# One core, matmul with RMS norm: four warming matmuls, and two products, two transposes, two block loads and two closing steps moved

## The chip, the cores and the metric

The kernel runs on one core of one Trainium2 chip. The metric is the device time of one execution in microseconds (us); the time before is the median of three runs. TensorE (PE) multiplies into eight PSUM banks, VectorE (DVE) and ScalarE (ACT) work on tiles in SBUF and read PSUM, GpSimd (POOL) issues the loads that change type, SyncE (SP) issues the stores and the DMA transposes.

## What is computed

```python
def reference(a, b, gamma, eps):          # a: 2048 x 2048, b: 2048 x 2048, fp32
    x = np.matmul(a, b)
    rms = np.sqrt(np.mean(x ** 2, axis=-1, keepdims=True) + eps)
    return (gamma * x / rms).astype(np.float32)
```

## The kernel before

Rows of A are cut into 16 blocks of 128, columns of B into four chunks of 512 (a left half and a right half, `j` = 0 and 1), the inner dimension into 16 tiles of 128, taken in 8 pairs (`kp`). The order of every engine's instructions is the order in which they are written, by hand: nothing is rescheduled. Each engine works through its own list and waits by semaphore for what another has to finish.

**Seven products for eight.** Two row blocks times one half of B make a 2 x 2 problem, which is done by a Strassen scheme of seven products, each 8 matmuls of 128x128 by 128x512 (`product`, L362; `product_matmul`, L350). Products 1, 2 use A's upper quarters, 4 its lower right one, 5, 6, 7, 3 use sums of quarters, numbered 1, 2, 3, 4 in `a_sums` (L328); B's sums are made by `b_diff` and `b_rest` (L340, L343). A product either starts a PSUM bank (1 and 7) or adds on top of what the bank holds. Between products that share a bank, ScalarE copies the bank to where the sum so far is wanted. Later groups do the same once more over two groups (`step`, L389).

**Stages.**
- Head: rows 0 to 3, left half, while B's left half streams in; plain matmuls (L406), A transposed on TensorE by `transpose_first` (L167) and `transpose_head` (L178). Ahead of it eight warming matmuls on zeros (L163).
- Right half of the head (`stream_right`, L472): rows 0 and 1 plain in acc[0] to acc[3] (`plain`), rows 2 and 3 (`PAIR`) by products: 1 and 6 and later 4 in `u2` = acc[4], 2 and 5 in `u4` = acc[5], 7 in `p7` = acc[6], 3 in acc[0]. B's last tile is used in the last step, `kp` = 7.
- Between (L515 to L561): the four banks of rows 0, 1 are evicted (L445); blocks 4 and 5 are normed on ScalarE (`row_norm`, L220), scaled to fp16 on VectorE (`row_factor`, `row_apply`, L230 to L243), turned on TensorE in two halves each (`transpose_half`, L191, into tbank and another bank) and copied out (`take_transposed`, L201). `pair_ends` (L556) then joins the banks of rows 2, 3: two ScalarE copies and three VectorE adds, the last of which reads acc[0].
- Groups of two blocks, 4 and 5 first: each half of each group is one segment, numbered `n`. `do(n, m)` (L572) issues product m and its copy, in the banks

```python
B1, B2, B3, B7 = (acc[1], acc[0]), acc[3:5], (acc[6], acc[5]), acc[2]
```

where the first index is `n % 2`: product 1 goes to B1, 4 and 6 to B2, 3 and 5 to B3, 7 to B7. `first_segment` (L607) is n = 0, `segment` (L638) and `block_segment` (L712) the next, `last_group` (L752) the blocks 14 and 15 together. `finish(r)` (L306) multiplies a row block by its inverse and gamma on VectorE and issues the store on SP. `square_half`, `square_right` (L275, L296) take the sums of squares on ScalarE.
- Blocks from 6 on are loaded by POOL (`load_block`, L132; two buffers), after a wait in POOL's own list (`wait_for`, L145), and `prepare` (L245) scales them on VectorE and turns them by DMA transposes on SP's queue.

Of the kernel before, what the change touches and what calls it, by code (L numbers as in the profile page):

```python
# [17 lines left out]
def kernel(  # L18
# [13 lines left out]
    nc = tc.nc  # L32
    P = 128
# [63 lines left out]
    def copy_on(engine):  # L97
        return nc.scalar.copy if engine == "A" else nc.vector.tensor_copy
# [60 lines left out]
    identity_h = consts.tile([P, P], FP16, name="identity_h")  # L159
    nc.vector.tensor_copy(out=identity_h, in_=identity_f)  # L160

    for _ in range(8):
        nc.tensor.matmul(acc[0], warm[:, 0:P], warm[:, 0:CH], start=True, stop=True)  # L163

    def transpose_first():  # L167
        bank = [tbank, acc[6]]
        view = [b.rearrange("p (r m) -> p r m", r=HB) for b in bank]
        for t in range(2):  # L170
            for r in range(HB):
                nc.tensor.matmul(view[t][:, r, :], a0f[:, r, t * P:(t + 1) * P], identity_f,
                                 is_transpose=True, start=(r == 0), stop=(r == HB - 1))
        for t, copy in enumerate((nc.vector.tensor_copy, nc.scalar.copy)):
            for h in range(2):
                copy(out=head_at[:, t, 2 * h:2 * h + 2, :], in_=view[t][:, 2 * h:2 * h + 2, :])
# [88 lines left out]
    def x_chunk(mb, c):  # L265
        return x_tile(mb, c // 2)[:, (c % 2) * CH:(c % 2 + 1) * CH]
# [94 lines left out]
    def product(g, j, m, bank, start=True):  # L361
        for kp in range(KP):  # L362
            product_matmul(g, j, m, bank, kp, start)
# [81 lines left out]
            copy_on(engine)(out=x_chunk(*g), in_=banks[g])  # L445

    transpose_first()
    for kp in range(KP):
        if kp + 4 < KP:
            load_head(kp + 4)  # L450
        else:
            load_later(1)
        before = [lambda: transpose_head(kp + 1)] if kp + 1 < KP else []
        if kp == KP - 2:
            before.append(lambda: a_sums(PAIR, (3,), False))
        stream(kp, before, len(groups1) + {0: 5, 1: 3}.get(kp, 2))
        if kp == KP - 1:
            evict(groups1, "ADADADA")
        stream_in_parts(last1, kp)
        if kp > 0:  # L460
            b_diff(0, kp - 1)
        if 0 < kp < KP - 2:
            b_rest(0, kp - 1)
# [8 lines left out]
    def stream_right(kp):  # L472
        first, second = ([(g, 2 * kp + t) for g in plain] for t in range(2))
        if kp == 0:
            for both in zip(first, second):
                for g, kt in both:
                    head_matmul(banks[g], *g, kt)
            product_matmul(PAIR, 1, 1, u2, kp, True)
            product_matmul(PAIR, 1, 2, u4, kp, True)
            return  # L480
        product_matmul(PAIR, 1, 1, u2, kp, True)
        for g, kt in first:
            head_matmul(banks[g], *g, kt)
        if kp == KP - 1:
            product_matmul(PAIR, 1, 7, p7, kp - 1, True)
        product_matmul(PAIR, 1, 2, u4, kp, True)
        if kp < KP - 1:
            product_matmul(PAIR, 1, 7, p7, kp - 1, True)
        for g, kt in second:
            head_matmul(banks[g], *g, kt)  # L490

    for kp in range(KP):
        load_later(1)
        b_diff(1, kp)
        stream_right(kp)
        if kp % 2 == 0:
            square_half(kp // 2, 0)
        if kp > 0:
            b_rest(1, kp - 1)
        if kp == 0:  # L500
            b_diff(0, KP - 1)
            b_rest(0, KP - 3)
        if kp == 1:
            b_rest(0, KP - 2)
            b_rest(0, KP - 1)
        if kp in (2, 3, 4):
            a_sums(PAIR, ((1,), (2,), (4,))[kp - 2])
# [4 lines left out]

    r2, r3 = HB - 2, HB - 1  # L515
    x11, x12, x21, x22 = (x_chunk(r, c) for r in (r2, r3) for c in (2, 3))
    copy_on("A")(out=x11, in_=u2)
    product_matmul(PAIR, 1, 7, p7, KP - 1, True)
    b_rest(1, KP - 1)
    add(x11, u4, x11)  # L520
    evict(plain[:1], "A")
    row_norm(HB)
    row_norm(HB + 1)
    product(PAIR, 1, 6, u2, start=False)
    nc.vector.tensor_copy(out=u4, in_=u2)
    row_factor(HB)
    row_apply(HB)
    evict(plain[1:2], "D")
    row_factor(HB + 1)
    row_apply(HB + 1)  # L530
    evict(plain[2:3], "A")
    product(PAIR, 1, 3, acc[0])
    product(PAIR, 1, 5, u4, start=False)
    turned = [transpose_half(HB, h, (tbank, acc[1])[h]) for h in range(2)]
    take_transposed(HB, 0, turned[0], nc.scalar.copy)
    take_transposed(HB, 1, turned[1], nc.vector.tensor_copy)
    load_block(HB + 3)
    for r in range(HB):
        take_pre(r)
    square_right(0)  # L540
    evict(plain[3:], "A")
    square_right(1)

    def turn(h):
        view = transpose_half(HB + 1, h, (tbank, acc[2])[h])
        take_transposed(HB + 1, h, view, nc.vector.tensor_copy)

    for kp in range(KP):
        if kp == 6:
            turn(0)  # L550
        product_matmul(PAIR, 1, 4, u2, kp, False)
    turn(1)
    load_block(HB + 4)
    a_sums(G0, (3, 1, 2), False)

    def pair_ends():  # L556
        nc.scalar.copy(out=x22, in_=p7)
# [49 lines left out]
    def first_segment():  # L607
        n, g, j = 0, G0, 0
        nxt = 2 * g + 2
        do(n, 1)  # L610
        do(n, 7, False)
        finish(0, (1,))
        pair_ends()
        do(n, 2)
        row_norm(nxt)
        a_sums(g, (4,))
        finish(0, (0,))
        do(n, 6)
        do(n + 1, 1)
        prepare(nxt)  # L620
        do(n, 5)
        nc.scalar.copy(out=chunks(n)[2], in_=B7)
        take(n, 22)
        row_norm(nxt + 1)
        take(n, 11)
        finish(1)
        do(n, 4)
        take(n, 21)
        prepare(nxt + 1)
        square_half(2 * g + 1, j)  # L630
# [7 lines left out]
    def segment(n):  # L638
        g, j = halves[n]
        ra, rb, nxt = 2 * g, 2 * g + 1, 2 * g + 2  # L640
        more = g + 1 < NG
        if g >= G2 and (g - G2) % 2 == 1 and j == 0:
            block_segment(n)
            return
        first = g >= G2 and (g - G2) % 2 == 0
        do(n, 6)
        if j == 0:
            finish(ra - 1)
            row_norm(nxt)
        elif g == G0:  # L650
            square_right(r2)
        do(n - 1, 3)
        take(n - 1, 12)
        if j == 0:
            square_right(ra - 2)
            prepare(nxt)
            a_sums(g, (4,))
            finish(ra - 2)
        else:
            if not first:  # L660
                square_half(ra, 0)
            if g == G0:
                square_right(r3)
                finish(r2, (1, 0))
            elif g == G0 + 1:
                finish(r3, (1,))
            elif g == G2:
                b_two(4)
            elif not first and g > G2:
                finish(ra - 2)  # L670
        if g < G2:
            do(n, 2)
            take(n, 11)
        if g == G2 - 1 and j == 1:
            b_two(3)
            b_two(1)
        do(n + 1, 1)
        if j == 1 and g + 2 < NG:
            wait_for(at(nxt + 1)[:, KT - 1, 0:1])
            if g > G0:  # L680
                load_block(nxt + 2)
                wait_for(a32[nxt + 2][:, 0:1])
            load_block(nxt + 3)
        if j == 1:
            if first:
                a_two_sums(g)
            a_sums(g + 1, (1, 2))
        do(n, 7)
        if j == 0:
            row_norm(nxt + 1)  # L690
        if j == 1:
            a_sums(g + 1, (3,))
        do(n, 5)
        take(n, 22)
        if j == 1:
            take_pre(rb)
            if not first:
                take_pre(ra)
        do(n, 4)
        take(n, 21)  # L700
        if j == 0:
            square_half(rb, 0)
            prepare(nxt + 1)
            if g == G2:
                b_two(2)
        else:
            if not first:
                square_right(rb)
            if g == G0:
                finish(r3, (0,))  # L710

    def block_segment(n):  # L712
# [11 lines left out]
        square_right(ra - 1)  # L724
        add(x00, W2, x00)
        prepare(nxt)
        do(n + 1, 1)
        take(n - 1, 12)
        square_half(ra - 2, 0)
# [22 lines left out]
    def last_group():  # L752
# [51 lines left out]
        do(n, 7)  # L804
        add(x22[0], x21[0], x22[0])
        add(b2[0], b2[0], x21[0])
        square_of(rb, x22[0])
        add(x11[1], x11[1], gam[2], ALU.mult)
        do(n + 1, 5)
        nc.scalar.copy(out=x22[1], in_=b3[1])  # L810
        wide = a_pool.tile([P, K], FP32, name="a32")
        chunk = [wide[:, c * CH:(c + 1) * CH] for c in range(NCH)]
        add(chunk[1], x22[0], gam[1], ALU.mult)
# [40 lines left out]
        r_b = inverse(root(last_sq, part))  # L854
        nc.vector.tensor_scalar_mul(out=xb[:, 0:CH], in0=xb[:, 0:CH], scalar1=r_b)
        nc.sync.dma_start(out=rows(rb, 0, CH), in_=xb[:, 0:CH])
        for c in (1, 3):
            by_r(chunk[c], r_b)
        scaled_gamma(chunk[2], b2[1], r_b, gam[2])
        nc.sync.dma_start(out=rows(rb, CH, N), in_=wide[:, CH:])  # L860

# [38 lines left out]
```

## Time and profile before

| what | value |
|---|---|
| median of three runs | 219.25 us (218.78 to 219.85) |
| the profiled execution | 219.36 us |
| its span, first to last instruction | 217.6 us |
| around the span | 1.76 us |
| mean granted TensorE clock | 0.990 |
| instructions | 2966 |
| first, last start of a TensorE matmul | 1.46, 210.18 us |
| HBM read, written | 34.60 MB, 16.78 MB |

A row of the timeline is: start, duration, engine, line and operation, output<-inputs, shapes, count, and in brackets how long the engine had been idle and what ended that. Rows of one kind that follow one another are merged (x8). PE is a matmul, PEld the load of its weights. A matmul of 512 columns is shown with 0.38 us, since its end is modelled; what it costs in a stream is the distance to the next start. "Who waited for whom" gives the engine and line, what it waited for, the sum, the count and the longest. In the row of slices, each digit is the busy share of a fortieth of the span in tenths.

### The profile page before, as it was taken

Reading aid. Unit: us, or ns where it says so; the run is one execution under the profiler, and the core shown is the slowest. Engines: PE = TensorE matmul, PEld = TensorE weight load, DVE = VectorE, ACT = ScalarE, POOL = GpSimd, SP = SyncE. Lnnn points to the kernel's source line nnn. Section 1 sums busy time; section 2 is a strip of 40 time slices with the busy share of each in tenths; the row PEclk is TensorE's granted clock in tenths of the full one; section 3 lists DMA queues with packets and bytes.
Section 4 is the critical chain, followed back from the end, with each engine's and each line's share of the span. In section 5 each row is a group of like instructions: output and inputs, shape, how many; then the busy total and the mean of one; then the engine's idle time right before and its main releaser. Section 6 shows DMA issues by size and latency. Waiting matters only on the chain.

```text
span 217.6 us, 2966 instructions
## 1 busy us (share of the span) xinstructions
PE 207.6 (95%) x1016; PEld 95.9 (44%) x1016; DVE 161.6 (74%) x323; ACT 113.3 (52%) x223; POOL 35.3 (16%) x74
## 2 busy tenths in 40 slices
PE   7899999999999999999999999999999999999970
PEld 3344544444455444444444444444444444444420
DVE  1227769999899997788975899399856985475771
ACT  2110001910599579498626962594728951555772
POOL 7644434434001000100021001100101000000020
PEclk9999999999999999999999999999999999999996
DMA  7999999999969798978674975497596992040454
GB/s 151 167 200 204 203 205 209 209 211 211 399 220 358 295 264 230 334 294 240 163 234 167 350 246 99 184 245 240 118 268 237 326 261 50 0 193 3 193 191 195
DMA packets 37039, 46.60 MB, mean 214 GB/s; under 512 B 22560, under 2 KB 26656, under 8 KB 35744
## 3 DMA queue, kind: packets, MB, share of 16 engines
q0 software_dynamic: 10608, 23.86, 45.5%
q1 hardware_dynamic: 26144, 22.29, 33.7%
q10 hardware_dynamic: 272, 0.26, 0.3%
q8 instruction: 8, 0.13, 0.2%
q14 instruction: 7, 0.06, 0.1%
HBM read 34.60 MB, written 16.78 MB: 236 GB/s over the span
## 4 chain that ended last, share of the span: by engine, by line
PE 85%; DMA 9%; POOL 2%; issue 1%; ACT 1%; ACTq 0%; DVE 0%; POOLq 0%
PE acc L358 65%; PE acc L406 11%; DMA early<-in_a_dram 5%; DMA b<-in_b_dram 4%; PE acc L397 3%; PE tbank L397 2%; POOL b L115 1%; PE tbank L358 1%; PE tbank L435 1%; PE tbank L182 1%; POOL early L119 1%; PE tbank L195 0%; PE acc L195 0%; ACT a L766 0%; ACTq L895 0%
## 5 line engine op out<-in xcount | busy, mean ns | idle before, releaser
L358 PEld LDWEIGHTS <-s 128*128 128x128 f16 (+1 forms) x312 | 30.5, 98 | 37.0 <-DVE s L335 0.3
L272 ACT ACTIVATE sq<-x 128x1024 bf16<-128x1024 f32 (+1 forms) x33 | 33.2, 1005 | 24.8 <-DVE x L101 20.9
L406 PE MATMUL acc<-b,head_at 128*128 128x512 bf16 x176 | 43.0, 379 | 0.9 <-DMA b<-in_b_dram 0.7
L311 DVE SCALAR_TENSOR_TENSOR x<-x,r,gamma_sb 128x1024 f32<-128x1024 f32 x28 | 34.9, 1282 | 0.5
L358 PE MATMUL acc<-b,head_at 128*128 128x512 bf16 x136 | 33.9, 379 | 0.0
L101 DVE TENSOR_TENSOR x<-acc,x 128x512 f32<-128x512 f32 x33 | 22.3, 687 | 11.4 <-PE acc L358 5.4
L358 PEld LDWEIGHTS <-head_at 128*128 128x128 f16 (+1 forms) x192 | 18.7, 98 | 22.2
L358 PE MATMUL acc<-b,at_even 128*128 128x512 bf16 x112 | 26.3, 379 | 0.0
L406 PEld LDWEIGHTS <-head_at 128*128 128x128 bf16 x176 | 16.9, 98 | 20.1 <-issue 1.0
L358 PE MATMUL acc<-early,s 128*128 128x512 bf16 x104 | 25.5, 379 | 0.0
L358 PE MATMUL acc<-b,s 128*128 128x512 bf16 x104 | 24.6, 379 | 0.0
L358 PEld LDWEIGHTS <-at_even 128*128 128x128 f16 x160 | 15.6, 98 | 18.6
L224 ACT ACTIVATE sq<-a 128x1024 bf16<-128x1024 f32 x22 | 23.3, 1058 | 0.6 <-DMA a<-in_a_dram 0.2
L358 PE MATMUL acc<-t_left,s 128*128 128x512 bf16 x96 | 22.7, 379 | 0.0
L115 POOL DMA_DIRECT2D b<-in_b_dram x32 | 17.2, 541 | 20.4 <-DMA b<-in_b_dram 14.3
L445 ACT COPY x<-acc 128x512 f32<-128x512 f32 x7 | 4.0, 581 | 25.8 <-PE acc L406 25.8
L587 ACT COPY acc<-acc 128x512 f32<-128x512 f32 x12 | 6.9, 576 | 10.4 <-PE acc L358 10.4
L187 DVE COPY head_at<-tbank 128x1024 bf16<-128x1024 bf16 x7 | 4.8, 691 | 8.1 <-PE tbank L182 8.1
L293 DVE RECIPROCAL r<-rms 128x1 f32<-128x1 f32 x16 | 2.6, 160 | 10.6 <-ACT rms L288 10.6
L101 DVE TENSOR_TENSOR x<-tbank,x 128x512 f32<-128x512 f32 x9 | 6.2, 690 | 4.2 <-PE tbank L435 4.1
L589 ACT COPY x<-acc 128x512 f32<-128x512 f32 x10 | 5.9, 585 | 5.3 <-PE acc L358 5.3
L769 POOL TENSOR_SCALAR x<-x,r 128x512 f32<-128x512 f32 x2 | 1.4, 691 | 41.9 <-DVE r L293 41.9
(129 smaller groups left out, 240.5 us busy)
## 6 DMA issues: line engine op xcount, KB each, us to landing
out_dram<-x SPq DMA_DIRECT2D x29, 512.0 KB, 3.0
a<-in_a_dram POOLq DMA_DIRECT2D x9, 1024.0 KB, 5.5
b<-in_b_dram POOLq DMA_DIRECT2D x32, 256.0 KB, 9.9
a<-in_a_dram POOLq DMA_DIRECT2D x4, 512.0 KB, 10.0
early<-in_a_dram POOLq DMA_DIRECT2D x7, 256.0 KB, 10.2
gamma_sb<-in_gamma_dram POOLq DMA_DIRECT2D x2, 512.0 KB, 10.1
head_at<-in_a_dram POOLq DMA_DIRECT2D x1, 1024.0 KB, 8.2
out_dram<-x SPq DMA_DIRECT2D x3, 256.0 KB, 2.6
```

What stands on the lines that cost most here:

```text
L101: nc.vector.tensor_tensor(out=out, in0=in0, in1=in1, op=op)
L115: nc.gpsimd.dma_start(out=raw[j][kp][:, t, :], in_=b[lo:lo + P, j * HALF:(j + 1) * HALF])
L187: nc.vector.tensor_copy(out=head_at[:, 2 * kp:2 * kp + 2, :, :], in_=view)
L224: nc.scalar.activation(out=junk, in_=a32[mb][:, h * HALF:(h + 1) * HALF], func=ACTF.Square, scale=2.0 ** -8, accum_out=n2[:, h:h + 1])
L272: nc.scalar.activation(out=sq[:, 0:src.shape[-1]], in_=src, func=ACTF.Square, scale=inv_sqrt_n, accum_out=msq[mb][:, c:c + 1])
L311: nc.vector.scalar_tensor_tensor(out=x, in0=x, scalar=inverse_of[mb], in1=gamma_sb[:, h * HALF:(h + 1) * HALF], op0=ALU.mult, op1=ALU.mult)
L358: nc.tensor.matmul(bank, lhsT[:, kp, :], rhs, start=(start and kp == 0), stop=(kp == KP - 1), skip_group_check=not start)
L397: nc.tensor.matmul(bank, lhsT[:, k, :], rhs, start=(m in (1, 7) and k == 0), stop=(k == KQ - 1), skip_group_check=m not in (1, 7))
L406: nc.tensor.matmul(bank, head_at[:, kt, r, :], head_rhs(c, kt), start=(kt == 0), stop=(kt == KT - 1))
L445: copy_on(engine)(out=x_chunk(*g), in_=banks[g])
L587: nc.scalar.copy(out=b3, in_=b2)
L589: nc.scalar.copy(out=chunks(n)[2], in_=B7)
```

## The change

1. Four more warming matmuls follow `transpose_first`.
2. In the last step of `stream_right`, product 6's first four matmuls, and the copy out of `u2` that they need, come ahead of product 2's last matmul, which uses B's last tile. The other four stay behind.
3. Product 4 of rows 2, 3 is issued in three parts: two matmuls ahead of block 4's transposes, four behind them, two behind block 5's transposes. VectorE scales block 5 behind its copy of block 4's second half; ScalarE evicts the last plain bank ahead of row 0's square.
4. Block 5's transposes, product 4's last part, block 8's load and the three sums of A go behind the first group's product 1; row 1's square goes there too. Product 2 of that group is issued ahead of product 7.
5. Block 14 is loaded as soon as block 12 is transposed, and normed and prepared one segment earlier, at the end of (g = 5, j = 1); block 15 takes block 14's old place in (g = 6, j = 0).
6. In `last_group` a square on ScalarE goes behind the copy that followed it, and two scalings of 512 columns become one instruction over both.

The counts of all other instructions are the same. The diff, without its context:

```diff
+    def busy(times):
+        for _ in range(times):
+            nc.tensor.matmul(acc[0], warm[:, 0:P], warm[:, 0:CH], start=True, stop=True)
+    busy(8)
...
     transpose_first()
+    busy(4)
...
         if kp == KP - 1:
+            copy_on("A")(out=x11, in_=u2)
             product_matmul(PAIR, 1, 7, p7, kp - 1, True)
+            for k in range(4):
+                product_matmul(PAIR, 1, 6, u2, k, False)
         product_matmul(PAIR, 1, 2, u4, kp, True)
...
-    copy_on("A")(out=x11, in_=u2)
...
-    product(PAIR, 1, 6, u2, start=False)
+    for kp in range(4, KP):
+        product_matmul(PAIR, 1, 6, u2, kp, False)
...
     row_factor(HB + 1)
-    row_apply(HB + 1)
     evict(plain[2:3], "A")
     product(PAIR, 1, 3, acc[0])
     product(PAIR, 1, 5, u4, start=False)
+    def product_4(lo, hi):
+        for kp in range(lo, hi):
+            product_matmul(PAIR, 1, 4, u2, kp, False)
+    product_4(0, 2)
     turned = [transpose_half(HB, h, (tbank, acc[1])[h]) for h in range(2)]
     take_transposed(HB, 0, turned[0], nc.scalar.copy)
     take_transposed(HB, 1, turned[1], nc.vector.tensor_copy)
+    row_apply(HB + 1)
     load_block(HB + 3)
     for r in range(HB):
         take_pre(r)
+    evict(plain[3:], "A")
     square_right(0)
-    evict(plain[3:], "A")
-    square_right(1)
-    def turn(h):
-        view = transpose_half(HB + 1, h, (tbank, acc[2])[h])
-        take_transposed(HB + 1, h, view, nc.vector.tensor_copy)
-    for kp in range(KP):
-        if kp == 6:
-            turn(0)
-        product_matmul(PAIR, 1, 4, u2, kp, False)
-    turn(1)
-    load_block(HB + 4)
-    a_sums(G0, (3, 1, 2), False)
+    product_4(2, 6)
+    def turn_next():
+        for h in range(2):
+            view = transpose_half(HB + 1, h, (tbank, acc[2])[h])
+            take_transposed(HB + 1, h, view, nc.vector.tensor_copy)
...
         do(n, 1)
+        square_right(1)
+        turn_next()
+        product_4(6, KP)
+        load_block(HB + 4)
+        a_sums(g, (3, 1, 2), False)
+        do(n, 2)
         do(n, 7, False)
         finish(0, (1,))
         pair_ends()
-        do(n, 2)
...
+        own = nxt + (g == NG - 2)
         if j == 0:
             finish(ra - 1)
-            row_norm(nxt)
+            row_norm(own)
...
-            prepare(nxt)
+            prepare(own)
...
-            if g > G0:
+            if G0 < g < NG - 3:
                 load_block(nxt + 2)
                 wait_for(a32[nxt + 2][:, 0:1])
             load_block(nxt + 3)
...
-        if j == 0:
+        if j == 0 and g < NG - 2:
             row_norm(nxt + 1)
         if j == 1:
             a_sums(g + 1, (3,))
+            if g == NG - 3:
+                row_norm(nxt + 2)
...
-            prepare(nxt + 1)
+            if g < NG - 2:
+                prepare(nxt + 1)
...
+            if g == NG - 3:
+                prepare(nxt + 2)
...
         prepare(nxt)
+        load_after(at(nxt)[:, KT - 1, 0:1], nxt + 2)
         do(n + 1, 1)
...
-        square_of(rb, x22[0])
         add(x11[1], x11[1], gam[2], ALU.mult)
         do(n + 1, 5)
         nc.scalar.copy(out=x22[1], in_=b3[1])
+        square_of(rb, x22[0])
...
-        for c in (1, 3):
-            by_r(chunk[c], r_b)
+        by_r(wide.rearrange("p (c n) -> p c n", n=CH)[:, 1::2, :], r_b)
```

## The prediction

> **What bounds the kernel now.** I read the page's shares first, then who waited on TensorE, the chain that ended last, and the timeline where the edits fall. Shares, and three of the slices:
>
> ```profile
> PE 207.6 (95%) x1016; PEld 95.9 (44%) x1016; DVE 161.6 (74%) x323; ACT 113.3 (52%) x223; POOL 35.3 (16%) x74
> PE   7899999999999999999999999999999999999970
> DVE  1227769999899997788975899399856985475771
> PEclk9999999999999999999999999999999999999996
> ```
>
> TensorE is full from the second slice to the last but one, at full clock; VectorE has long full stretches too. All that TensorE waited for:
>
> ```profile
> PE acc L163 <- DVE pace L155: 1.5, 1, 1.5
> PE acc L406 <- DMA b<-in_b_dram: 0.7, 1, 0.7
> PE tbank L435 <- DVE head_at L187: 0.4, 1, 0.4
> PE tbank L182 <- DMA early<-in_a_dram: 0.2, 1, 0.2
> ```
>
> The last of these is at 26.02 us. In the chain:
>
> ```profile
> 15.19 10.79 DMA early<-in_a_dram
> ...
> 67.09 70.79 PE acc L358 x328
> ```
>
> So the kernel is input DMA up to 26.02, then matmuls one behind the other (216 ns a step, 1.726 for a product of eight) up to 210.6, with one hole that the list is too coarse for (203.49, below), then 7 us of ending. An edit between 26 and 210 can gain almost nothing; it can only open a hole. The question at each is what still covers it.
>
> **Part 1, four more warming matmuls.** The first head matmuls run 6.11 to 7.78 and the next waits until 8.51 for B (the 0.7 above). Four at 216 ns are 0.86: they start near 5.85, so the seven head matmuls run 6.72 to 8.23 and still meet the wait. Cost 0, cover left 0.28. At half clock (427 ns, as the warming ones at 1.46 to 4.85) they are 1.71, less the hole of 1.1 between 7.41 and 8.51: at most 0.6. Below nothing: a hole of 1.1 left the clock at full, so nothing is saved here.
>
> The Trainium skill's page "TensorE: Matmul & The Clock Gate", Part 1, speaks against this edit: the gate opens after about 3.4 us of sustained work, in a window that runs free, so more matmuls behind an open gate buy nothing. The trace agrees: granted clock 1.00 in every stretch from 10 us on. By the row the four cost 0, by the rule with the gate a window later the 0.6 above. The same section closes the gate after an idle window of about 3.4 us; the stall of part 4 is shorter, so by the rule it costs no clock either.
>
> **Part 2, half of product 6 ahead.** It needs its bank copied first: ScalarE's copy (L517) runs 56.06 to 56.65 and the moved matmuls start at 56.94. Cover 0.29, cost 0. B's last tile is then needed 4 x 216 ns = 0.86 later. VectorE starts on that tile at 56.64 and TensorE at 56.94: no wait to remove here. But the head matmuls end 0.86 later, so ScalarE's eviction and both row norms do: norm 4 ends at 61.58 (60.71), norm 5 at 64.13 (63.27). VectorE's block 4 scaling then ends at 63.60 (62.87), after block 4's transposes began (63.42); two matmuls of product 4 put ahead move those to 63.85. Cost 0; without that cover 0.2.
>
> **Part 3, block 4.** The first group's product 1 writes the bank of the second turned half. That half's transposes start at 64.30 and end at 64.91; VectorE's copy runs 64.95 to 65.64, now ahead of block 5's scaling. TensorE arrives, after four more matmuls of product 4, at 64.74 + 0.86 = 65.61 and goes on 0.05 after the copy (as at L435: copy to 11.21, matmul at 11.26), at 65.69. Cost **0.08**. Queued behind the copy is block 5's scaling, to 66.85; its transposes are now wanted at 67.42, so it is covered.
>
> **Part 4, block 5 behind product 1, 2 ahead of 7.** This is where I see a new wait. Product 1 of the next half (n = 1) starts in acc[0], where product 3 of rows 2, 3 lies until `pair_ends`' last add (72.83 below):
>
> ```profile
> 66.48 0.61 PE L195 MATMUL acc<-identity_h,a_first 128*128 128x128 f16 x8
> ...
> 67.13 0.69 DVE L202 COPY at_even<-acc 128x1024 f16<-128x1024 f16 x1
> 67.86 0.69 DVE L335 TENSOR_TENSOR s<-at_even 128x1024 f16<-128x1024 f16 x1
> ...
> 68.59 0.69 DVE L335 TENSOR_TENSOR at_even<-at_even 128x1024 f16<-128x1024 f16 x1
> ...
> 69.31 0.69 DVE L335 TENSOR_TENSOR s<-at_even 128x1024 f16<-128x1024 f16 x1
> ...
> 70.11 1.28 DVE L311 SCALAR_TENSOR_TENSOR x<-x,r,gamma_sb 128x1024 f32<-128x1024 f32 x1
> ...
> 72.83 0.69 DVE L101 TENSOR_TENSOR x<-acc,x 128x512 f32<-128x512 f32 x1
> ...
> 73.84 1.46 PE L358 MATMUL acc<-b,at_even 128*128 128x512 bf16 x6
> ```
>
> From the start of the second half's transposes (66.48), VectorE needs 0.65 to its copy, then copy, three sums, reciprocal, a finish of row 0 and three adds, all back to back, to 73.52: with 0.05 of release 7.09. TensorE has 0.45 of transposes and four products (1, 7, 2, 6), 7.36, and arrives 0.27 late enough. After the change VectorE's list is the same, but product 1 stands before the transposes: TensorE has 0.44 + two matmuls 0.43 + three products 5.18 = 6.05. VectorE needs 0.28 more, since both halves are turned back to back and the second copy queues behind the first (68.07, then 68.80 where its half is ready at 68.52): 7.37. Stall 7.37 - 6.05 = **1.32**, at about 73.9 to 75.2. Bounds: 1.04 without the queueing; 1.7 if block 5's scaling or a copy slips by 0.4, the longest single idle that ScalarE's and VectorE's rows of this stretch note (0.28 to 0.42). Behind the waiting matmul stand products 5, 4 and their copies, all later alike. VectorE comes out 0.27 later against TensorE, which its idle 0.96 at 84.53 takes back. Product 7 wants the first sum at 70.47 and it is done near 70.2; product 6 wants the third at 72.19, done near 71.7: covered. The DMAs: block 6's load is issued near 64.3 (63.41, landing 5.1 later), wanted at 70.5; block 7's near 67.4, lands 73.4, wanted at 78.4; block 8's waits for product 4's last matmul, 69.1, lands 77.3, wanted near 95. All covered.
>
> **Part 5, blocks 14, 15 prepared earlier.** Block 14's load moves from 156.81 to behind block 12's transposes (issued 145.53, 3.2 to landing), near 149; it took 7.5 us, so it lands near 156.5. Its row norm is now wanted on ScalarE at 160.1, in an idle 3.65 that holds its 2.7; its scaling falls into VectorE's 1.60 of idle before 165.25. On SP the two transposes go ahead of two outputs that no one waits for soon. TensorE waited nowhere here, so nothing is gained; cost 0, up to 0.5 if the load crosses block 13's transposes and the norm holds ScalarE.
>
> **Part 6, the end.**
>
> ```profile
> 202.24 0.63 ACT L272 ACTIVATE sq<-x 128x512 bf16<-128x512 f32 x1 [1.57 <-DVE x L101]
> ...
> 202.87 0.57 ACT L810 COPY x<-acc 128x512 f32<-128x512 f32 x1
> ...
> 203.49 3.12 PEld L358 LDWEIGHTS <-s 128*128 128x128 f16 x15 [0.27 <-issue]
> ...
> 211.95 1.33 ACT L766 ACTIVATE a<-a,r 128x512 f32<-128x512 f32 x2 [0.28 <-DVE r L293]
> 212.30 0.74 DVE L762 SCALAR_TENSOR_TENSOR a<-acc,r,gamma_sb 128x512 f32<-128x512 f32 x1
> ...
> 213.31 0.33 SPq L860 DMA_DIRECT2D out_dram<-a x1
> ```
>
> The copy of L810 stood behind a square that waited for VectorE; product 3 of the last half needed that copy and came at 203.49, where 203.34 was due (0.22 after the matmul at 203.12). With the copy first: **-0.15**. The two scalings of 1.33 become one of 1024 elements. ScalarE's squares cost 1.06 at 1024 and 0.63 at 512, so 0.43 for 512 more: 0.73 + 0.43 = 1.16, **-0.17** ahead of the last output's issue (bounds -0.25, where VectorE's 213.04 takes over, and 0).
>
> **Sum.** 0.08 + 1.32 - 0.15 - 0.17 = +1.08. The profiled execution took 219.36 (span 217.6 and 1.76 around it): 220.44. It lies 0.11 above the median shown, 219.25, from which it would be 220.33. I say 220.4. About 0.5%, 1.1 us, is what a measurement of this kernel can tell from no change, and the forecast lies on that bound: it is slower or just not told apart.
>
> **Rivals.** (a) *The stall is not there, so the change is not slower.* Place: acc[0] before product 1 of n = 1. If VectorE gets through in 6.05 or less, only 0.08 - 0.32 = -0.24 is left: 219.1. For it: a margin of 0.27 stands there now, so the order was near balance. Against it: the rows stand back to back with no idle noted, and VectorE gets no work less. Chance 0.13. (b) *A second hole.* ScalarE held at block 14's norm, or the warming matmuls at half clock: another 0.5 to 1, 221.4. The rows give covers of 0.28 to 3.6, hence 0.12. (c) *Input later in the timed runs than in this one*, which span 1.07: B's last tile is 0.30 ahead of its use, and the change adds 0.86 of room. With (a) besides: 219.25 - 0.24 - 0.86 = 218.15. Chance 0.07. The stall alone has 0.68.
>
> **Numbers.** The stall case gives 219.9 to 221.1, a little over half of it above the bound: slower 0.39, same 0.29. With (b) slower 0.51; with (a) same 0.42; (c) faster 0.07. The range goes from (a) to the upper bounds of stall and warming: 219.0 to 221.6.
>
> **What would show it.** A wait of TensorE for VectorE's add (L101) of about 1.3 us near 74, none in the profile before; no gap in the last half's product 3; one scaling row of about 1.16. Wrong if TensorE runs through 74 without a hole, if another hole is longer, or if the clock falls behind the stall.

## The result, and the profile after

The changed kernel takes 221.22 us (median of 22 runs, 219.9 to 222.21), beside 219.54 for the kernel before in the same session (22 runs, 218.78 to 221.83). The ratio is 1.0058, with a 95% interval of 1.0036 to 1.008: slower, by 0.0058 x 219.54 = 1.27 us. The two medians lie further apart, 1.68, and a second set of runs (9, below) gave 1.0085, or 1.86. By these values the loss is 1.3 to 1.9 us; the forecast was +1.08, 220.4.

The profiled execution took 220.88 us with a span of 219.1; before it was 219.36 and 217.6. So it is 1.52 longer, and the span 1.5. First the page's shares, and the three slices that were shown of before:

```profile
PE 208.7 (95%) x1020; PEld 97.1 (44%) x1020; DVE 161.6 (74%) x323; ACT 112.9 (52%) x222; POOL 36.0 (16%) x74
PE   7999999999999899999999999999999999999970
DVE  1227779999887997789975899399758883385771
PEclk9999999999999999999999999999999999999995
```

The shares say nothing: 95% stands in both, and the four added matmuls are most of PE's longer busy time. One slice of PE has fallen to 8, the fourteenth, 71 to 77 us. The clock stays at full. The list of TensorE's waits says more (total, times, longest one):

```profile
PE acc L361 <- DVE x L101: 1.6, 2, 1.1
PE acc L164 <- DVE pace L155: 1.5, 1, 1.5
PE tbank L438 <- DVE head_at L190: 0.3, 1, 0.3
```

The two waits for input (0.7 and 0.2) are gone, and at the top stands a wait that before did not have: `product`'s matmul for VectorE's add, L101, **twice**. The timeline of TensorE and VectorE around the first (start, duration, line, tile):

```profile
65.26 1.28 DVE L246 TENSOR_SCALAR a_first<-a,s 128x2048 f16<-128x2048 f32 x1
65.40 1.89 PE L361 MATMUL acc<-b,at_even 128*128 128x512 bf16 x8
...
67.57 0.61 PE L198 MATMUL acc<-identity_h,a_first 128*128 128x128 f16 x8
67.84 0.69 DVE L205 COPY at_even<-tbank 128x1024 f16<-128x1024 f16 x1 [1.02 <-PE tbank L198]
...
68.44 0.68 DVE L205 COPY at_even<-acc 128x1024 f16<-128x1024 f16 x1
...
70.17 3.62 PE L361 MATMUL acc<-t_left,s 128*128 128x512 bf16 x16
...
71.41 1.28 DVE L314 SCALAR_TENSOR_TENSOR x<-x,r,gamma_sb 128x1024 f32<-128x1024 f32 x1
...
74.13 0.69 DVE L101 TENSOR_TENSOR x<-acc,x 128x512 f32<-128x512 f32 x1
...
74.87 3.61 PE L361 MATMUL acc<-b,at_even 128*128 128x512 bf16 x16 [1.08 <-DVE x L101]
```

TensorE's last matmul ahead of it started at 73.41 and the next one at 74.87: 1.46 apart where a step is 0.216, a **hole of 1.25**. VectorE ends its last add at 74.82 and the matmul starts 0.05 later, with the copies, the finish of row 0 (71.41) and the adds back to back ahead of it. This is the stall of the forecast.

The second one stands at 176.55, and the forecast gave that place no cost of its own. ScalarE, VectorE and TensorE there, by their timelines:

```profile
167.78 1.06 ACT L227 ACTIVATE sq<-a 128x1024 bf16<-128x1024 f32 x1 [1.10 <-DMA a<-in_a_dram]
...
170.47 0.15 DVE L235 TENSOR_SCALAR s<-norm 128x1 f32<-128x1 f32 x1 [1.05 <-ACT norm L230]
...
173.42 2.48 DVE L314 SCALAR_TENSOR_TENSOR x<-x,r,gamma_sb 128x1024 f32<-128x1024 f32 x2
...
174.15 1.89 PE L361 MATMUL acc<-early,s 128*128 128x512 bf16 x8
...
175.82 1.48 DVE L101 TENSOR_TENSOR x<-acc,x 128x512 f32<-128x512 f32 x2
176.55 1.89 PE L361 MATMUL acc<-b,s 128*128 128x512 bf16 x8 [0.51 <-DVE x L101]
```

Read it downward: ScalarE waits 1.10 for block 15's load, VectorE 1.05 for ScalarE's norm, TensorE for VectorE's add. Start to start TensorE has 892 ns here (its last matmul before began at 175.66), a hole of 0.68. Before the change block 15's load was issued later, but its norm (171.12 below) stood behind the landing, at 170.41, and TensorE went on without a wait:

```profile
164.96 0.53 POOL L137 DMA_DIRECT2D a<-in_a_dram  x1 [0.37 <-ACT sq L272]
...
171.12 1.07 ACT L224 ACTIVATE sq<-a 128x1024 bf16<-128x1024 f32 x1
...
174.85 1.89 PE L358 MATMUL acc<-b,s 128*128 128x512 bf16 x8
```

Upstream of the hole in the changed kernel, POOL and SP:

```profile
151.04 0.53 POOL L137 DMA_DIRECT2D a<-in_a_dram  x1
...
160.04 0.70 POOL L146 CAST pace<-at_even 128x1 f32<-128x1 f16 x1 [8.47 <-DMA at_even<-a]
160.69 0.53 POOL L137 DMA_DIRECT2D a<-in_a_dram  x1
```

```profile
152.44 1.24 SPq L253 DMA_TRANSPOSE at_even<-a_half  x1
153.85 3.31 SPq L253 DMA_TRANSPOSE at_even<-a  x1
```

The first load is block 14's, now early; it lands at 157.31. Block 13's two transposes are issued into it, at 152.44 and 153.85, and land at 159.11 and 159.92: 6.7 and 6.1 us. Before, no load was in flight there, and they took 3.4 and 3.15. The profile's line for these two transposes, before and after:

```profile
DMA to landing us min/median/max: 3.1/3.3/3.4
```

```profile
DMA to landing us min/median/max: 6.1/6.4/6.7
```

POOL's copy of L146 (`wait_for`) waits for the second of them, and only then may it issue block 15's load, at 160.69, which lands at 167.76. The norm of block 15 was moved up to block 14's old place, where ScalarE is free for it at 166.68, 1.10 ahead of that landing.

The account of the profiled executions, by starts of matmuls: everything ahead of product 4 and block 4's transposes 0.29 earlier (63.42 to 63.13), by less waiting for input, product 1 of the first group +0.08, the stall +1.25, the second hole +0.68, the gap in the last product 3 (0.15) gone. That is +1.57; the last matmul starts at 211.73 for 210.18, +1.56. Behind it the merged scaling:

```profile
213.50 1.15 ACT L784 ACTIVATE a<-a,r 128x1024 f32<-128x1024 f32 x1 [0.28 <-DVE r L296]
...
214.68 0.33 SPq L877 DMA_DIRECT2D out_dram<-a  x1
```

1.15 us for the former 1.33; the last output's issue is 1.37 later than before. The profile's line for that output, before and after:

```profile
DMA to landing us min/median/max: 3.3/3.3/3.3
```

```profile
DMA to landing us min/median/max: 3.5/3.5/3.5
```

So the output is issued 0.19 nearer to the last matmul (2.94 behind its start, not 3.13) and lands no nearer: 6.40 behind it, not 6.42.

### The profile page after: what moved, and what is told of

Same layout as the page of the kernel before. It is cut to its first block, busy times and chain, and to the rows that moved or that the text cites. A ratio compares the mean times of both kernels' runs of the same rounds, so it can differ in the third digit from the quotient of the medians.

```text
span 219.1 us, 2974 instructions
## 1 busy us (share of the span) xinstructions
PE 208.7 (95%) x1020; PEld 97.1 (44%) x1020; DVE 161.6 (74%) x323; ACT 112.9 (52%) x222; POOL 36.0 (16%) x74
## 4 chain that ended last, share of the span: by engine, by line
PE 72%; DMA 13%; DVE 8%; issue 3%; ACT 2%; POOL 0%; ACTq 0%; DVEq 0%; POOLq 0%
PE acc L361 50%; PE acc L409 14%; DMA early<-in_a_dram 4%; DMA a<-in_a_dram 3%; DMA at_even<-a 3%; PE acc L400 3%; DMA b<-in_b_dram 2%; DVE x L101 2%; PE tbank L400 2%; DVE x L314 1%; PE tbank L438 1%; PE tbank L185 1%; ACT sq L227 1%; DVE s L338 1%; PE tbank L361 1%
## 5 line engine op out<-in xcount | busy, mean ns | idle before, releaser
L101 DVE TENSOR_TENSOR x<-acc,x 128x512 f32<-128x512 f32 x33 | 22.3, 687 | 12.2 <-PE acc L361 6.3
L101 DVE TENSOR_TENSOR x<-tbank,x 128x512 f32<-128x512 f32 x9 | 6.2, 692 | 4.2 <-PE tbank L438 4.1
```

The source lines that it names most:

```text
L101: nc.vector.tensor_tensor(out=out, in0=in0, in1=in1, op=op)
```

## The experiments

My theory after the result: the time is the wait for `acc[0]` plus the second hole, which the preparation of blocks 14 and 15 makes. Rivals: the later VectorE list or TensorE's own order would cost the same without that wait; the second hole is only the first one's delay handed on; some smaller part pays.

**Ratios below are to the kernel before, run beside it on the same chip, with their 95% intervals. Holes are the distance between starts of matmuls in the profiled execution, less a step (0.216; 0.056 behind a transpose).**

**1. The wait alone.** The finish of row 0, 1.28 us of VectorE, goes behind the adds that free `acc[0]`:

```
         do(n, 7, False)
-        finish(0, (1,))
         pair_ends()
+        finish(0, (1,))
```

> The changed kernel, with the finish of row 0's right half put behind the three adds that free acc[0], nothing else moved. Theory (VectorE's list is too long ahead of acc[0]): the list up to the last add loses the reciprocal and the finish, some 1.4 us of the rows (71.22 to 72.61), so the add ends near 72.8 and TensorE comes at 73.6: the hole of 1.25 at 73.41 is gone, the one of 0.68 at 175.66 stays, time 1.2 below the changed kernel's, about 0.1 to 0.3 above the kernel before. Rival (VectorE as a whole is behind, the place of the wait is chance): the hole comes back within the next segment, some 1 us of it, and the time stays within 0.4 of the changed kernel's.

Measured: 220.02 us, ratio 0.9997 (0.997 to 1.0025). VectorE, and TensorE's matmuls on either side:

```profile
72.89 0.69 DVE L101 TENSOR_TENSOR x<-acc,x 128x512 f32<-128x512 f32 x1
...
73.69 1.28 DVE L314 SCALAR_TENSOR_TENSOR x<-x,r,gamma_sb 128x1024 f32<-128x1024 f32 x1
```

```profile
70.33 3.62 PE L361 MATMUL acc<-t_left,s 128*128 128x512 bf16 x16
73.78 3.62 PE L361 MATMUL acc<-b,at_even 128*128 128x512 bf16 x16
```

Sixteen steps of 0.216 from 70.33 are 73.78: no hole. The finish (73.69) now runs behind the adds, and nothing waits for it: the order of two statements carried the stall. The second hole stayed, 0.82 behind the matmul at 174.58, so it is not the first one handed on.

**2. Blocks 14, 15 in their old places**, in the changed kernel:

```
-        own = nxt + (g == NG - 2)
...
-            row_norm(own)
+            row_norm(nxt)
...
-            if G0 < g < NG - 3:
+            if g > G0:
...
-        load_after(at(nxt)[:, KT - 1, 0:1], nxt + 2)
```

(`prepare` and the guarded norms go back in the same way.)

> The changed kernel with part 5 undone: blocks 14 and 15 are loaded, normed and prepared where they were before. Theory (block 14's early load crosses block 13's transposes, block 15's load and norm come late, VectorE's finish ahead of the add that product 3 waits for comes late): the hole of 0.68 at 175.66 is gone, the one of 1.25 at 73.41 stays, block 13's transposes land 3.2 after issue and not 6, time 0.6 to 0.7 below the changed kernel's. Rival (the hole comes from the shift that the first hole leaves, not from the blocks): the hole stays at about 0.7.

Measured: 221.7 us, 1.0102 (1.0068 to 1.0135): not 0.65 below the changed kernel (1.0058, and 1.0085 in run 9) but level with it or above, which the intervals leave open. Of TensorE's waits:

```profile
PE acc L361 <- DVE x L101: 1.1, 1, 1.1
...
PE acc L361 <- DMA head_at<-a_half: 0.4, 1, 0.4
```

The second wait for VectorE is gone, as expected. In its place TensorE waits for block 14's transposes, a hole of 0.54 ahead of 178.41, and has 0.12 more ahead of 185.44. Block 13's transposes, with no load beside them, landed 4.0 and 3.5 after their issue. The mechanism was confirmed and the price was missed, because I had taken the old places, the load's among them, as free.

**3. Both at once.**

> Both edits at once: the finish behind the adds, and part 5 undone. Theory: both holes are gone, 1.25 + 0.68 = 1.9 below the changed kernel, and against the kernel before 0.08 more at product 1 and 0.33 less at the end: about 0.25 faster than before, which a few rounds hardly tell. Rival (the two holes are not the whole of the loss, the start or the moved product 6 cost too): it stays 0.5 or more above the kernel before.

Measured: 222.4 us, 1.0116 (1.0059 to 1.0172). No wait for `acc[0]`, and yet slower. The six runs go from 220.7 to 223.73; the profile is of one of the two fastest, 220.75, and what the other four have besides, no profile shows. TensorE:

```profile
177.40 1.90 PE L361 MATMUL acc<-b,head_at 128*128 128x512 bf16 x8 [0.76 <-DMA head_at<-a_half]
...
185.05 1.90 PE L361 MATMUL acc<-t_left,s 128*128 128x512 bf16 x8 [0.56 <-DVE s L338]
```

Holes of 0.92 and 0.73. Block 15's load runs 165.91 to 172.41 and block 14's transposes, issued at 169.75, land at 177.36: 7.6 us. Before, that load ran 164.96 to 170.41 and the transposes took 4.3, from 169.84 to 174.18. With a load one microsecond later and one longer, they took three more. Why the load came later is seen further up, on VectorE and POOL:

```profile
155.13 2.48 DVE L314 SCALAR_TENSOR_TENSOR x<-x,r,gamma_sb 128x1024 f32<-128x1024 f32 x2
...
156.47 1.19 POOL L146 CAST pace<-at_even 128x1 f32<-128x1 f16 x1 [15.83 <-DMA at_even<-a]
...
157.59 0.53 POOL L137 DMA_DIRECT2D a<-in_a_dram  x1
```

That copy took 0.35 before, and block 14's load went out at 156.81; block 15's load waits for block 14's. Here the copy began 0.14 behind the start of the second of VectorE's two finishes and ended 0.05 behind its end (157.61); before, it began in the first and ended 0.04 behind that one's end (156.57). Kernel 2 shows the same, 1.22 us. In all fourteen profiles together, each of the 43 such copies of 0.35 or more ended 0.04 to 0.05 behind a VectorE instruction with two inputs in SBUF, and the 55 others took 0.18 to 0.19, some of them beside VectorE adds that read PSUM. That points to VectorE as what held the copy up; no run changes that alone.

The early load of block 14 is thus also a cover: it keeps block 15's load off block 14's transposes.

**4. The end alone** (part 6 on the kernel before).

```
-        square_of(rb, x22[0])
...
         nc.scalar.copy(out=x22[1], in_=b3[1])
+        square_of(rb, x22[0])
...
-        for c in (1, 3):
-            by_r(chunk[c], r_b)
+        by_r(wide.rearrange("p (c n) -> p c n", n=CH)[:, 1::2, :], r_b)
```

> The kernel before with part 6 alone: the square behind the copy, and one scaling for two. Theory: no gap at the last half's product 3 (0.15) and the last store issued 0.18 earlier: 0.3 faster than before. Rival (the last store's landing is set by the store ahead of it or by the DMA engines): the store is issued earlier and lands no earlier, 0.15 or less.

Measured: 219.18 us, 0.9981 (0.9959 to 1.0004). The gap at 203 is gone and the scaling takes 1.15. But the last output, issued 0.19 sooner behind the last matmul, lands 6.42 behind its start, as before: the rival is right, and 0.15 is what part 6 has in the trace. In all fourteen profiles, three of them without part 6, that landing is 6.40 to 6.42; what holds it there no run shows. In the times the gain is 0.4, with an interval that includes no gain. The profiled execution itself (219.44) has holes of 0.19, 0.16 and 0.22 elsewhere, the last for the sums behind block 15's transposes.

**5. Early load kept, norms of 14 and 15 in their old places**, and the finish behind the adds: edit 1, and of edit 2 all but its last two parts.

> The changed kernel with the finish behind the adds, with block 14's early load kept, but with the norms and preparations of blocks 14 and 15 in their old places. Theory (the early load only moves the crossing of a load with transposes to block 13, which has room; the hole of 0.68 to 0.82 near 175 comes from block 15's norm standing where block 14's stood, ahead of VectorE's finish): block 13's transposes still take 6 us to land, block 14's land in 3 to 4, no hole near 175 and none at block 14's first product (which undoing the load opened, 0.5 to 0.9): 0.8 below e1_finish_behind, 0.5 to 1.0 faster than before. Rival (the crossing itself costs, wherever the norms stand): a hole of 0.5 or more stays between 165 and 186.

Measured: 219.26 us, 0.9996 (0.9975 to 1.0017). Every wait of TensorE that the profile lists:

```profile
PE acc L164 <- DVE pace L155: 1.5, 1, 1.5
PE tbank L438 <- DVE head_at L190: 0.3, 1, 0.3
```

Neither hole is left. Block 13's transposes still took 6.7 and 6.0, and block 14's 4.6 and 4.0. So the late transposes alone cost nothing: the norm of block 15, placed ahead of its load's landing, is what handed them to TensorE (its place and block 14's were put back together). The size was missed: I expected 0.5 to 1.0 below the kernel before and it came out level. What is left in the trace, 0.08 at product 1 against 0.15 at the end, is too small to be told.

**6. Half of product 6 ahead, alone** (part 2 on the kernel before).

```
+            copy_on("A")(out=x11, in_=u2)
             product_matmul(PAIR, 1, 7, p7, kp - 1, True)
+            for k in range(4):
+                product_matmul(PAIR, 1, 6, u2, k, False)
...
-    copy_on("A")(out=x11, in_=u2)
...
-    product(PAIR, 1, 6, u2, start=False)
+    for kp in range(4, KP):
+        product_matmul(PAIR, 1, 6, u2, kp, False)
```

> The kernel before with part 2 alone. Theory (the head matmuls end 0.86 later, so both row norms and block 4's and 5's scalings do, and parts 3 and 4 are what covers it): holes of about 0.2 ahead of block 4's transposes and 0.6 ahead of block 5's, no wait at B's last tile, 0.5 to 0.8 slower than before. Rival (part 2 is free on its own and gives room for B's last tile): no hole of 0.2 or more between 56 and 70, time the same or up to 0.4 faster.

Measured: 219.81 us, 1.0016 (1.0004 to 1.0028), +0.35. TensorE has holes of 0.23 ahead of block 4's transposes (63.68), 0.14 ahead of their second half (64.28) and 0.21 ahead of block 5's (66.23), where 0.6 was expected. The first is the "0.2 without that cover" of the forecast; in the changed kernel, with product 4's and block 5's new places, none of the three appears.

**7. The warming matmuls** (kernel 5 without `busy(4)`).

> As e5_behind_early, without the four added warming matmuls. Theory (they stand beside the wait for B's second half and cost and give nothing): the same as e5_behind_early within 0.3, with a hole of 0.7 to 1.1 back near 8 and first block of matmuls at the same time after 12. Rival (they delay the head when the clock opens late, or they keep the clock): 0.3 to 0.6 faster, or slower, than e5_behind_early.

Measured: 219.32 us, 1.0007 (0.9985 to 1.003), beside 0.9996 for kernel 5 on the same chip: worth nothing that can be told. Its profiled execution has holes of 0.5 ahead of 44.94, for B, and of 0.5 ahead of 60.33, for VectorE's sums of B's last tile.

**8. The early load alone** (on the kernel before).

```
-            if g > G0:
+            if G0 < g < NG - 3:
...
+        load_after(at(nxt)[:, KT - 1, 0:1], nxt + 2)
```

> The kernel before with block 14's early load alone (norms and preparations where they were). Theory (in the profile before block 14's transposes land 1.4 ahead of their use, and block 15's load, which they cross, decides whether that holds; the runs before reach up to 222): the early load takes block 15's load out of the way, block 14's transposes land in 3.5 or less, the median falls by 0 to 0.5 and the highest runs by more. Rival (the early load costs as much at block 13): a hole of 0.3 or more between 155 and 165, slower than before.

Measured: 219.14 us, 0.9996 (0.9972 to 1.002). Block 14's transposes landed 3.4 and 3.1 us after their issue; no gain, and one run still took 221.8. Block 13's transposes, which nothing but the load beside them changed, took 5.7 and 5.2 where they had taken 3.4 and 3.15, and no hole of 0.3 followed: the rival did not come.

**9 to 12, on one chip**: the changed kernel again, kernels 1 and 5 again, and early load and end together on the kernel before.

> The changed kernel itself, beside the two that follow on one chip, to see what each hole is worth in timed runs. Theory (two holes of 1.25 and 0.7, less 0.25): 1.3 to 1.7 above the kernel before, the holes at 73 and 175 as before. Rival (the second hole is of that one profiled execution): 1.0 above, one hole.

> e1_finish_behind again, same chip. Theory: 1.2 below e12_changed_again; if the second hole is in the timed runs, 0.3 to 0.6 above the kernel before. Rival (the second hole is not in most timed runs): as fast as the kernel before or 0.2 faster.

> e5_behind_early again, same chip. Theory (second hole real, and gone here): 0.6 to 0.8 below e10_finish_again and 0.2 to 0.4 faster than before. Rival: within 0.2 of e10_finish_again.

> The kernel before with part 6 and block 14's early load, nothing of parts 1 to 4. Theory (part 6 is worth 0.33, the early load nothing in most runs, and parts 1 to 4 only move waits about): 0.3 to 0.5 faster than before, equal to or 0.2 faster than e11_early_again. Rival (parts 2 to 4 give room for late input that this one lacks): slower than e11_early_again by 0.3 or more.

| kernel | us | ratio (95%) | holes in its profile |
|---|---|---|---|
| changed | 221.14 | 1.0085 (1.0061 to 1.0109) | 0.08, 1.25 ahead of 75.27, 0.44 ahead of 176.72 |
| finish behind | 219.93 | 1.0025 (1.0007 to 1.0043) | 0.08, 0.77 ahead of 175.34 |
| finish behind, norms in old places | 219.17 | 0.9997 (0.9986 to 1.0009) | 0.08, 0.52 ahead of 59.90 |
| before, with early load and end | 219.09 | 0.999 (0.9971 to 1.0008) | none from 172 to 186 |

Each step down takes one hole away. In the timed runs the first is worth 0.0060 or 1.32 us, beside 1.25 in the trace, and their intervals stand apart. The second is worth 0.0028 or 0.61, beside 0.44 to 0.82 in the profiles; these two intervals just meet, and between kernels 1 and 5 as first run the times showed no such step. The hole is sure by the trace, its price only about. The second hole as kernel "finish behind" has it, and the same place without it:

```profile
172.84 1.89 PE L361 MATMUL acc<-early,s 128*128 128x512 bf16 x8
175.34 1.89 PE L361 MATMUL acc<-b,s 128*128 128x512 bf16 x8 [0.61 <-DVE x L101]
```

```profile
173.34 1.89 PE L361 MATMUL acc<-early,s 128*128 128x512 bf16 x8
175.07 1.89 PE L361 MATMUL acc<-b,s 128*128 128x512 bf16 x8
```

2.50 from product to product in the one, 1.73, eight steps, in the other.

None of the gains of 0.2 to 0.5 that were expected is shown. No version was shown to be faster than the kernel before: the lowest ratios, 0.9981 and 0.999, have intervals that take in 1, and I did not separate them.

## Why the prediction was right, and where it was not

The forecast's case was the stall alone, and the stall came, in the place named and of about the size. It did not come alone. The terms:

- **Part 1, 0.** Right. Taken away, nothing changes that can be told (run 7). The head matmuls stayed at full clock.
- **Part 2, 0, with 0.2 without its cover.** Right in the change. Alone it costs 0.35 by the times and 0.59 of holes in the trace, so the cover was worth two to three times what I gave it.
- **Part 3, 0.08.** Exact: 297 ns from start to start where a step is 216.
- **Part 4, 1.32.** 1.25 in the trace, 1.32 between the timed runs with and without it. The cause was tested by moving one statement: with the finish of row 0 behind the adds, VectorE's list as a whole is as long, and the hole is gone. The margin that I had worked out, 7.37 against 6.05, contained that finish, 1.28 of it.
- **Part 5, 0, "up to 0.5 if the load crosses block 13's transposes and the norm holds ScalarE".** This step failed. The load did cross them, but the norm that waited was block 15's, not block 14's, and the cost was 0.68. I had followed block 14's load and its norm and not the next step: POOL's wait for block 13's second transpose stands ahead of block 15's load. The forecast also had block 14's load near 149, with 3.2 from issue to landing for block 12's transposes; the row of before gives 3.65 (145.53 to 149.18), and the load was issued at 151.04. Nor was it true that nothing is gained here since TensorE waited nowhere: runs 2 and 3 show that in the changed kernel the old place of block 14's load cost 0.54 and 0.92 at block 14's transposes, and 0.12 and 0.73 close behind.
- **Part 6, -0.15 and -0.17.** The first is right: the gap is gone. The second failed: the row is 1.15 where 1.16 was estimated and the output is issued 0.19 sooner, but it lands no sooner behind the last matmul (6.40, before 6.42), so this term is 0.02.
- **The sum.** +1.08 was forecast; +1.27 was measured by the first ratio and +1.86 by the second. In the profiled execution the unforeseen 0.68 was partly offset by input that came 0.29 earlier. That offset is the executions' and was not a term of mine: the four profiles with the head of before reach that place at 62.99 to 63.42, the eight with the changed head at 63.06 to 63.56. Without it the terms of the trace (0.08 + 1.25 + 0.68 - 0.15) give +1.86. So the largest term and its mechanism were right, and that the first ratio came within 0.2 of the sum is partly luck: it lacks a term of 0.68 and has one of -0.17 that did not come.

Of the rivals, (a) is refuted: VectorE did not get through in time. (b) came half true, a second hole of 0.68, but by block 15's load and not by either road named. (c) did not come: no version was shown to be faster. Its room of 0.86 was wrong in part. Half of product 6 wants the last B tile later, but the sums of VectorE on that tile feed product 6's last matmul at the same time as before, and in one execution those were late by themselves:

```profile
59.90 0.38 PE L361 MATMUL acc<-early,s 128*128 128x512 bf16 x1 [0.36 <-DVE early L101]
```

That is the third kernel of the table: the single matmul came at 59.90 behind one at 59.16, a hole of 0.52.

**The clock.** It stayed open through the stall of 1.25, at a granted 1.00 from 6.37 us to the end of the matmuls. That agrees with the Trainium skill, "TensorE: Matmul & The Clock Gate", Part 1, by which a gate closes only after a longer idle window.

## What to carry to other kernels

When an accumulator bank goes back into use earlier, list everything that stands on the freeing engine ahead of its last read: one statement of 1.28 us that nobody waited for, put behind the read, took the whole stall of 1.25 away. When a load is moved, follow the queue behind it one step further than the load itself, to the transposes that it meets, to the waits that stand for those, and to the next load. A place in the order where no one waits can still be the cover of another; undo such a part alone before calling it free.

## What was not expected of the hardware

- DMA transposes issued into a load of 1 MB took 5.0 to 7.6 us from issue to landing; block 13's took 3.1 to 3.4 in the profile before, with none in flight, and 5.2 to 5.7 when that load alone was added (run 8). The Trainium skill, "DMA: Bandwidth & Descriptors", section "Issuing engines are not separate DMA queues", has all engines' DMAs on the same 16 engines, interleaved. The longer time agrees with that; which packets stood in front of which, no run here shows.
- The same eight warming matmuls brought the clock to full at 5.04 us in the profiled execution before and at 6.37 in the one after; over all profiled executions it was 4.49 to 6.40.
- POOL's wait copy of one element per partition took from 0.18 to 1.22 us, and it stands ahead of a load. Every one of 0.35 or more ended with a VectorE instruction that reads two inputs from SBUF; in run 3 that was a finish of 1.28, and the load behind the copy went out 0.78 later than before.
